# First weights prepared in the opening stage, weight work spread over iterations, and mLSTM products in the last four iterations of an attention loop

## The chip, the cores and the metric

One core of a Trainium2 chip runs one launch of the kernel. The metric is device time in microseconds: the median of three runs before the change is 1974.31 (1969.93 to 1977.7). Smaller is better.

## The reference

The reference is one layer of a diffusion backbone: 1024 latent tokens and 256 context tokens, 1024 channels. What matters here is its first half. A normalised and modulated `h` is projected once; the parts feed two token mixers, and a sigmoid gate weighs each:

```
h  = modulate(rms_norm(x, norm1_w), sh1, sc1);  hc = the same for ctx
aq, ak, av, mq, mk, mv, mo, mg, ga, gm = split(h @ w_in)
att = windowed_gqa(rope(norm(aq)), rope(norm(ak)), av, k_ctx, v_ctx, sink)   # 16 heads, 4 KV heads, window 128
ml  = readout(bidirectional mLSTM(mq, mk, mv, gates mg; states from ctx), mo) # 4 heads, chunks of 128
y   = sigmoid(ga) * (att @ w_branch_att) + sigmoid(gm) * (ml @ w_branch_ml)
x   = x + g1 * (y @ w_out);  then a convolutional SwiGLU with its own residual
```

All of it is fp32. The kernel holds fp32 accuracy on TensorE by splitting an operand in a high and a low half and taking three products: high by high, high by low, low by high.

## The kernel before, in words

The stages run one after another: `stage_startup` (modulation vectors, context projections, and `h` in transposed halves `hH`, `hL`), `stage_attention`, `stage_mlstm`, and a tail with the merge and the feed-forward part. Outside the attention loop a planner sets the order of instructions on each engine with its own cost model; `tc.issue_after(x)` makes what follows on an engine stand behind `x`. The attention loop is under `tc.manual_schedule()`: there each engine runs in the order written, and a wait on one instruction holds all that is behind it on the same engine. Loads of weights all go through SP's queue, in order too.

**Weights.** A weight becomes two 16-bit halves in four steps (class `ScaledWeights`, L84 to 159): load of fp32 quarters (`raw`, L100), squares summed on ACT (`square`, L111), a total across partitions by a product with ones on PE, a reduction on DVE, a scale with a power on POOL (`total`, L118 to 121; `back`, L125 and L126), and the split, on POOL in three instructions for each piece: scale (L140), cast (L141), subtract (L142). A group's attention weight has four quarters of 128x768 (the first 128x800), a gate weight two halves of 128x512.

**Attention loop.** Its 36 iterations `n` are a pipeline over 32 pairs (group of heads `g` = n // 8, block of 128 tokens `b`). In iteration n, the projection `pq` of pair n (24 products, L686), the transposes of pair n-1 (L772), the scores, maxima, exponentials and low halves of pair n-3 (four heads; L822 to L825 on PE, L830 and L846 on DVE, L838 to L841 on ACT), and the value products `po` of pair n-4 stand interleaved. Between them stand 24 products of a gate tile `g` (j = 0 at n = 0, then j = n - 2 up to 31, two tiles for each of 16 gate weights). In an iteration, DVE reduces the squares of `pq` (L717 on ACT, L724 on DVE) to row factors, POOL finishes them (L725 to L727), DVE rotates the key by them (L750), POOL adds (L761, L762). `pv_end` (L887, POOL) multiplies the finished output by norms that come back from DRAM (`R`). The reciprocals of the softmax sums are transposed on PE (L861, `norm_turn`), ahead of the gate products.

The weight work has its own timetable in the loop. Gate weight c is loaded at the end of iteration 2c - 1, squared in 2c, totalled in 2c + 1, and both halves are split in 2c + 1; its first tile is due in 2c + 2. The attention weight of group g = 1 to 3 is loaded in iterations 8(g-1) and 8(g-1) + 2, squared in the iterations after each, totalled at n % 8 = 4, and split two quarters there and two at n % 8 = 6. `weight_back` (L642) also makes scalars for the values on POOL and takes a reciprocal on DVE (L654). Before the loop, the first attention weight and the first gate weight go through all four steps, and the loop's first projection and gate tile wait for them. In iterations 32 to 35 there is no projection, in 34 and 35 no gate tile.

**mLSTM start.** `prepare(0)` loads, squares and totals the weights `w_ml` and `w_mlqo` of head 0, `gate_math` is a chain of small operations for the gates (from L1219 to L1313), `load_kv(0)` splits `w_ml` on ACT and DVE, `proj_kv(0)` makes keys and values `kv` for eight latent blocks (24 products each, L162 to L164), and `trans_k`, `states` (L1365 on), `proj_q` and `core` follow.

Of the kernel before, what the change touches and what calls it, by code (L numbers as in the profile page):

```python
# [18 lines left out]
P = 128  # L19
D = 1024  # L20
# [69 lines left out]
class ScaledWeights:  # L90
# [4 lines left out]
    def __init__(self, E, tc, ctx):  # L95
        self.E, self.nc = E, E.nc
        pool = lambda name, bufs: ctx.enter_context(tc.tile_pool(name=name, bufs=bufs, reuse_waits="tile"))
        self.rp, self.hp, self.lp, self.sp = pool("w2_raw", 4), pool("w2_h", 8), pool("w2_l", 8), pool("w2_s", 1)

# [239 lines left out]
def stage_startup(E, at):  # L339
# [3 lines left out]
    with ExitStack() as st:  # L343
# [28 lines left out]
        def norm(i, t, late=None):  # L372
            junk = wp.tile([P, D], F32, tag="junk", name=f"xj{i}", bufs=1)
# [189 lines left out]
        for i in range(4):  # L563
# [6 lines left out]
            for k in range(0, KT, 2):  # L570
# [8 lines left out]
                if i == 1 and k < 4:  # L579
                    for c in range(2 * k, 2 * k + 4, 2):  # L580
                        X[4 + c // 2] = load(NCB + 4 + c // 2)
            if i == 2:
                at.tables(cs)
# [18 lines left out]
def stage_attention(E, st, at):  # L602
# [12 lines left out]

    norm_d = E.dr.tile([NKV * NB, 512], F32, name="norm_d")
# [6 lines left out]
    WSRC = [(A["w_att0"], 400)] + [(A["w_att"][g], 384) for g in range(3)]  # L623
# [19 lines left out]
    def weight_back(g):  # L643
        f = RAW["wf", g]
        w2.back(f)
# [11 lines left out]
    def gate_load(c, i):  # L657
        raw = fp.tile([P, 4, P], F32, tag="fr", name=f"fr{c}_{i}")
# [283 lines left out]
    for k2 in range(4):  # L942
        weight_load(0, k2)
        weight_square(0, k2)
    weight_total(0, tp_tile("wt0"))
    weight_back(0)
    for k2 in range(4):
        weight_split(0, k2)
    for i in range(2):
        gate_load(0, i)  # L950
        gate_square(0, i)
    gate_total(0, tp_tile("gt0"))
    gate_back(0)
    for i in range(2):
        gate_split(0, i)
    for i in range(2):
        mod_fetch()

    def squares(n, i):
        if n % 2 == 0 and 1 <= n // 2 < 16:  # L960
            gate_square(n // 2, i)
        if n % 8 in (1, 3) and n // 8 < 3:
            weight_square(n // 8 + 1, n % 8 - 1 + i)

    prior, tile_done, out_done = None, None, None
    with tc.manual_schedule():
        for n in range(LAST):
# [5 lines left out]
            if tile_done:  # L973
                gate_act(*tile_done)
# [3 lines left out]
            squares(n, 0)  # L978
# [8 lines left out]
            ps, new = proj(*now) if now else (None, Products())  # L987
# [5 lines left out]
            if n % 8 == 6 and n // 8 < 3:  # L993
                weight_split(n // 8 + 1, 2)
                weight_split(n // 8 + 1, 3)
# [9 lines left out]
            new.some(len(new.todo))  # L1005
            if prior:
                prior.norm_turn(pt[0:4, 384:512])
            c = n // 2 if n % 2 and 1 <= n // 2 < 16 else None
            if c:
                gate_total(c, ps[:, 448:])  # L1010
            heavy = n // 8 + 1 if n % 8 == 4 and n // 8 < 3 else None
            if heavy:
                weight_total(heavy, ps[:, 448:])
            j = TILES.get(n)
            fps, gate = gate_tile(j) if j is not None else (None, Products())
            gate.some(8)
# [5 lines left out]
            if c:  # L1022
                for i in range(2):
                    gate_split(c, i)
            if heavy:
                weight_split(heavy, 0)
# [4 lines left out]
            sq = values_act(*now, ps) if now else None  # L1031
# [15 lines left out]
            if c:  # L1047
                gate_back(c)
            if heavy:
                weight_back(heavy)  # L1050
                weight_split(heavy, 1)
# [4 lines left out]
            squares(n, 1)  # L1056
            gate.some(24)
            if j is not None:
                tile_done = j, fps
# [14 lines left out]
            if n % 2 and 1 <= (n + 1) // 2 < 16:  # L1074
                for i in range(2):
                    gate_load((n + 1) // 2, i)
            if n % 8 in (0, 2) and n // 8 < 3:
                for i in range(2):
                    weight_load(n // 8 + 1, n % 8 + i)
            prior = S  # L1080
        if tile_done:
            gate_act(*tile_done)
# [1293 lines left out]
```

## Time and profile before

| what | us |
|---|---|
| median of the runs shown | 1974.31 |
| the profiled execution, its own time | 1971.89 |
| its span, first to last instruction | 1969.9 |
| first and last L717 (one for each projection) | 119.6, 637.3 |
| first and last attention product (L686) | 102.5, 697.3 |
| PE, DVE, ACT, POOL busy, share of the span | 93%, 72%, 54%, 25% |
| mean granted TensorE clock | 0.969 |

PE's busy share is the mean of stages with different limits, and matmuls are pipelined, so it is not PE at its peak. POOL's 25% lies nearly all in the first third of the span. The chain of waits that ended last runs over PE for 67% of the span.

### The profile page before, as it was taken

The page shows a single profiled execution, that of the slowest core. Times are in us where ns is not written, and L with a number is a line of the kernel's source. Part 1 is how long each engine was busy: PE and PEld are TensorE (multiplying, and loading weights), DVE is VectorE, ACT ScalarE, POOL GpSimd, SP SyncE. Part 2 cuts the span into 40 slices and gives each one's busy share as a digit, 9 for nine tenths or more (in the row PEclk, how much of TensorE's full clock was granted, in tenths as well). Part 3 has the DMA queues.
Part 4 walks back from the last instruction along what each step waited for, and adds up shares of the span by engine and source line. Part 5 has one row for each costly group of instructions (what it writes and reads, how often), then busy time and mean ns, then how long its engine had stood idle before and what let it go on. Part 6 is the DMA issues. An engine that isn't in the chain of part 4 may idle for free.

```text
span 1969.9 us, 27867 instructions
## 1 busy us (share of the span) xinstructions
PE 1826.1 (93%) x9121; PEld 1318.9 (67%) x9121; DVE 1423.7 (72%) x2874; ACT 1069.9 (54%) x2199; POOL 493.7 (25%) x739
## 2 busy tenths in 40 slices
PE   7858888988899789999999999999999999999999
PEld 4824554545555446565656888787888888888887
DVE  3826766766767657586768778769998988997565
ACT  4716666666667655656445656246544444454441
POOL 2476647647554224131302002000000000000000
PEclk9979999999999889999999999999999999999999
DMA  9625775777767770516243993632355444489851
GB/s 353 194 80 118 158 154 122 158 161 149 162 145 156 157 216 22 182 63 208 74 150 112 371 346 101 244 130 76 124 186 204 181 169 168 166 305 354 293 180 64
DMA packets 301936, 342.46 MB, mean 174 GB/s; under 512 B 175824, under 2 KB 200416, under 8 KB 298976
## 3 DMA queue, kind: packets, MB, share of 16 engines
q1 hardware_dynamic: 287392, 314.47, 52.7%
q10 hardware_dynamic: 14400, 26.22, 4.1%
q8 instruction: 72, 1.18, 0.3%
q14 instruction: 72, 0.59, 0.1%
HBM read 224.61 MB, written 76.16 MB: 153 GB/s over the span
## 4 chain that ended last, share of the span: by engine, by line
PE 67%; ACT 7%; DMA 7%; POOL 7%; DVE 6%; issue 5%; SPq 1%; ACTq 0%; POOLq 0%; DVEq 0%
PE g L686 5%; PE pa L1954 4%; PE pa L1956 4%; PE pa L1955 4%; PE pq L686 4%; PE po L686 3%; DMA fr<-in_w_g 2%; PE dx L1954 2%; PE dx L1956 2%; PE dx L1955 2%; PE pb L1956 2%; PE pb L1955 2%; PE pb L1954 2%; PE yb L1954 2%; PE yb L1956 2%
## 5 line engine op out<-in xcount | busy, mean ns | idle before, releaser
L830 DVE CUSTOM_DVE_ANT_0 s<-s,maskA,nsink 128x640 f32<-128x640 f32 (+1 forms) x128 | 117.3, 916 | 78.9 <-PE s L825 78.4
L846 DVE TENSOR_TENSOR P<-s,P 128x640 f16<-128x640 f32 (+1 forms) x128 | 100.6, 786 | 25.9 <-ACT s L841 25.7
L686 PE MATMUL pq<-wha,hH 128*128 128x384 f16 (+1 forms) x256 | 90.1, 352 | 31.2 <-DVE t L750 18.5
L686 PE MATMUL g<-hH,fh 128*128 128x512 f16 x256 | 102.3, 400 | 3.1 <-POOL fh L141 3.1
L840 ACT ACTIVATE P<-s,st 128x640 f16<-128x640 f32 (+1 forms) x128 | 98.2, 768 | 8.5 <-DMA T<-P 4.0
L686 PE MATMUL g<-hH,fl 128*128 128x512 f16 x256 | 101.6, 397 | 0.6 <-POOL fl L142 0.6
L686 PE MATMUL g<-hL,fh 128*128 128x512 f16 x256 | 102.1, 399 | 0.0
L686 PE MATMUL pq<-wla,hH 128*128 128x384 f16 (+1 forms) x256 | 89.5, 350 | 4.7 <-POOL wla L142 4.7
L841 ACT ACTIVATE s<-s,st 128x640 f32<-128x640 f32 (+1 forms) x128 | 93.9, 734 | 0.0
L686 PEld LDWEIGHTS <-hH 128*128 128x128 f16 x512 | 51.2, 104 | 63.6 <-issue 21.1
L162 PE MATMUL kv<-whkv,hH 128*128 128x384 f16 x256 | 85.3, 333 | 4.8 <-DVE VL L56 4.8
L686 PE MATMUL pq<-wha,hL 128*128 128x384 f16 (+1 forms) x256 | 89.5, 349 | 0.0
L838 ACT ACTIVATE st<-st,shift 128x1 f32<-128x1 f32 x128 | 37.2, 291 | 94.9 <-DVE st L830 94.5
L822 PE MATMUL s<-KA,QT 128*128 128x384 f32 (+1 forms) x128 | 64.1, 501 | 25.3 <-DVE P L846 16.7
L163 PE MATMUL kv<-wlkv,hH 128*128 128x384 f16 x256 | 85.2, 333 | 0.4
L164 PE MATMUL kv<-whkv,hL 128*128 128x384 f16 x256 | 84.9, 331 | 0.0
L686 PEld LDWEIGHTS <-fh 128*128 128x128 f16 x512 | 49.6, 104 | 51.5 <-issue 7.8
L1365 POOL TENSOR_SCALAR kwh<-k,gcall 128x128 fp32r<-128x128 f32 x72 | 32.1, 450 | 177.6 <-PE dC L163 72.7
L2092 ACT ACTIVATE cv<-ua,vecT 128x1024 f32<-128x1024 f32 x22 | 27.4, 1245 | 85.3 <-DVE ua L2065 85.3
L1954 PE MATMUL dx<-dwh,dfh 128*128 128x512 f32 (+1 forms) x176 | 68.3, 388 | 0.0
L1956 PE MATMUL dx<-dwh,dfl 128*128 128x512 f32 (+1 forms) x176 | 68.3, 388 | 0.0
L1955 PE MATMUL dx<-dwl,dfh 128*128 128x512 f32 (+1 forms) x176 | 68.2, 387 | 0.0
(670 smaller groups left out, 6204.1 us busy)
## 6 DMA issues: line engine op xcount, KB each, us to landing
ur<-in_w_up SPq DMA_DIRECT2D x22, 1024.0 KB
wmb<-in_w_modB SPq DMA_DIRECT2D x48, 256.0 KB
f_d<-cv SPq DMA_DIRECT2D x22, 512.0 KB
wm<-in_w_modA SPq DMA_DIRECT2D x16, 512.0 KB
fr<-in_w_g SPq DMA_DIRECT2D x32, 256.0 KB
drf<-fs_d SPq DMA_DIRECT2D x15, 512.0 KB
drw<-wt_d SPq DMA_DIRECT2D x14, 512.0 KB
w1b<-in_w_cx SPq DMA_DIRECT2D x16, 388.0 KB
```

The costliest lines, as they stand in the source:

```text
L162: nc.tensor.matmul(ps, lh[:, ls], rh[:, rs], start=start and i == 0, stop=False)
L163: nc.tensor.matmul(ps, lh[:, ls], rl[:, rs], start=False, stop=False)
L164: nc.tensor.matmul(ps, ll[:, ls], rh[:, rs], start=False, stop=stop and i == n - 1)
L686: nc.tensor.matmul(self.ps, x, w, start=self.i == 0, stop=self.i == self.n - 1)
L822: nc.tensor.matmul(s[:, self.lat], q, G[g]["KA"][:, ks], start=True, stop=False)
L830: nc.vector.tensor_tensor_reduce(e, e, self.mask, scale=self.ss[:, h : h + 1], scalar=nsink[:, hh : hh + 1], op0=ALU.add, op1=ALU.min, acc ...
L840: nc.scalar.activation(two[:, :W], e, AF.Exp, bias=m, scale=-1.0)
L841: nc.scalar.activation(e, e, AF.Exp, bias=m, scale=-1.0, accum_out=st4[:, 4 + h : 5 + h])
L846: nc.vector.tensor_tensor(two[:, W : 2 * W], self.e[h], two[:, :W], op=ALU.subtract)
L1954: nc.tensor.matmul(ps, lh, rh, start=start and i == 0, stop=False, skip_group_check=True)
L1955: nc.tensor.matmul(ps, lh, rl, start=False, stop=False, skip_group_check=True)
L1956: nc.tensor.matmul(ps, ll, rh, start=False, stop=stop and i == n - 1, skip_group_check=True)
```

## The change

- `stage_startup`: the first attention weight's loads are traced in step 1 of the context loop, its squares there too, its total and its POOL splits at the start of step 2 (splits behind the last norm factor). The first gate weight is loaded in step 2, squared there and totalled in step 3. The rotary tables move from the end of step 2 to the end of step 1. The norms' junk tile is 16 bit.
- Before the loop: only the scalars of group 0, the splits of gate weight 0, three gate loads and one weight load are left.
- In the loop each piece has its own iteration. Gate weight c: loads at the end of 2c - 5 and 2c - 4, squares in 2c - 3 and 2c - 2, total in 2c - 1, splits in 2c and 2c + 1. Group g, with a = 8(g-1): loads in a - 1 to a + 2, squares in a + 1 to a + 4, total in a + 4, splits in a + 5 to a + 8; the last quarter stands at the head of POOL's work in its iteration, the other pieces behind `pv_end`.
- `w_ml` and `w_mlqo` of head 0 join the timetable: `w_ml` as a fifth group (split in 29 to 32), `w_mlqo` loaded in 30 to 33, squared in 32 to 35, totalled in 35.
- `norm_turn` moves behind the first eight gate products.
- In iterations 32 to 35 the place of the projection, and in 34 and 35 that of the gate tile too, is taken by the 24 products of one of the mLSTM's blocks 0 to 5; ACT copies the result to SBUF (`kv0`, held until `proj_kv(0)` is done), and `proj_kv(0)` reads it from there. Blocks 6 and 7 stay.

```diff
@@ stage_startup, context loop (step i, piece k)
+                w2 = E.w2
+                if i == 1 and k == 2:
+                    E.raw0 = [w2.raw(A["w_att0"][:, j : j + 2, :], 400, f"a0_{j // 2}") for j in range(0, KT, 2)]
+                if i == 1 and k == 4:
+                    q0 = w2.sums("a0")
+                if i == 1 and k >= 4:
+                    for j in (k - 4, k - 3):
+                        w2.square(q0, j, E.raw0[j], "a0")
+                if i == 2 and k == 0:
+                    E.f0 = w2.total(q0, 4, tp_tile("wt0"), "a0")
+                    w2.back(E.f0)
+                    E.W0 = []
+                    with tc.issue_after(E.factor.ins):
+                        for j in range(4):
+                            h, lo = w2.halves(400, f"a0_{j}")
+                            w2.split_pool(E.raw0[j], E.f0, h, lo)
+                            E.W0 += [(h[:, jj], lo[:, jj]) for jj in range(2)]
...
+            if i == 1:
+                at.tables(cs)
             if i == 2:
-                at.tables(cs)
                 context_squares()
@@ stage_attention
+    def early(j, ps):
+        todo = [
+            (x[:, sl(j * P, P)], w)
+            for (xh, xl), (wh, wl) in zip(hT, W1[NKV])
+            for x, w in ((xh, wh), (xh, wl), (xl, wh))
+        ]
+        return ps, Products(ps[:, :384], todo)
+
+    def early_act(j, ps):
+        E.kv0[j] = E.kvp.tile([P, 384], F32, name=f"kv0_{j}")
+        copy_act(nc, E.kv0[j], ps[:, :384], scale=RAW["wf", NKV][:, 4:5])
+
+    def gate_slots(c):
+        load = [2 * c - 5, 2 * c - 4]
+        square = [max(2 * c - 3, 0), 2 * c - 2]
+        return load, square, 2 * c - 1, [2 * c, 2 * c + 1]
+
+    def weight_slots(g):
+        if g > NKV:
+            return [30, 31, 32, 33], [32, 33, 34, 35], 35, []
+        a = 8 * (g - 1)
+        return [a + k - 1 for k in range(4)], [a + k + 1 for k in range(4)], a + 4, [a + k + 5 for k in range(4)]
...
-            ps, new = proj(*now) if now else (None, Products())
+            splits = list(jobs(n, 3))
+            for kind, c, i in splits:
+                if kind == "w" and i == 3:
+                    weight_split(c, i)
+            ps, new = proj(*now) if now else early(n - N, mm_tile(f"kv0_{n - N}"))
...
+            elif n >= N + 2:
+                fps, gate = early(n - N + 2, E.fl_tile(f"kv0_{n - N + 2}"))
+            gate.some(8 if valued != seq[-1] else 24)
             if prior:
                 prior.norm_turn(pt[0:4, 384:512])
@@ stage_mlstm, proj_kv
+            elif h == 0 and j - NCB in E.kv0:
+                kv = E.kv0[j - NCB]
+                copy_act(nc, k, kv[:, 0:DQK], scale=DQK ** -0.5)
+                vs[j] = v_tiles(h, j, kv[:, 128:384])
```

More of the change, by code (lines that the diff above doesn't have):

```diff
@@ L622, in stage_attention @@
     w2 = E.w2
-    WSRC = [(A["w_att0"], 400)] + [(A["w_att"][g], 384) for g in range(3)]
+    WSRC = [(A["w_att0"], 400)] + [(A["w_att"][g], 384) for g in range(3)] + [(A["w_ml"][0], 384), (A["w_mlqo"][0], 384)]
     def weight_load(g, k2):
@@ L1021, in stage_attention @@
                 mod_sum()
[L1022 to L1026, printed above, removed]
             if S:
@@ L1046, in stage_attention @@
                 context_values(g)
[L1047 to L1051, printed above, removed]
+            for kind, c in totals(n):
+                (gate_back if kind == "g" else weight_back)(c)
             if S:
```

122 lines of the change are left out of this document (75 added, 47 removed).

## The prediction

> **What bounds the kernel now.** I read the windows first (busy time by stretch), then who waits for whom, then the timelines where a stretch loses time. In a windows row the fields are: stretch, its length, busy us (and instructions) of PE, PEld, DVE, ACT, POOL, then granted clock, DMA share and GB/s.
>
> ```profile
> 73.00:81.00 8.00, 6.84 (x42) 6.24 (x42) 7.71 (x8) 6.44 (x11) 8.00 (x8) 1.00 0.81 216
> 81.00:93.00 12.00, 12.00 (x76) 11.85 (x75) 8.86 (x15) 10.47 (x19) 0.21 (x1) 1.00 0.56 185
> 93.00:110.00 17.00, 4.90 (x21) 2.37 (x20) 4.38 (x11) 2.85 (x6) 14.82 (x17) 0.70 0.46 129
> 110.00:130.00 20.00, 10.89 (x32) 4.18 (x32) 3.13 (x12) 0.64 (x2) 19.30 (x22) 0.66 0.04 14
> 590.57:604.21 13.64, 13.64 (x79) 8.56 (x78) 11.12 (x29) 11.01 (x29) 4.86 (x8) 1.00 0.83 153
> 572.34:590.57 18.23, 16.60 (x88) 9.98 (x86) 11.10 (x32) 11.05 (x28) 11.48 (x14) 0.91 0.65 131
> 188.00:647.00 459.00, 402.80 (x2147) 241.29 (x2145) 314.85 (x803) 299.83 (x746) 274.98 (x345) 0.96 0.71 151
> 647.00:698.00 51.00, 36.73 (x147) 20.30 (x147) 31.97 (x69) 30.47 (x68) 9.26 (x17) 0.74 0.73 160
> 698.00:753.00 55.00, 49.28 (x278) 28.33 (x276) 29.41 (x83) 32.72 (x79) 15.91 (x45) 0.96 0.53 167
> ```
>
> Three places lose PE time. From 93 to 130 POOL is full and PE mostly waits: POOL alone splits the first weights. In the loop, two neighbouring iterations of the same work take 13.64 and 18.23; the fast one keeps PE busy all the time, so 13.64 is PE's own pace. And from 647 to 698, where the projections have ended, PE works 36.73 of 51 at clock 0.74.
>
> ```profile
> 72.71 0.55 POOL L384 TENSOR_TENSOR rs<-ss,expo 128x1 f32<-128x1 f32 x1
> 73.23 0.20 POOL L321 TENSOR_SCALAR nsink<-sink 128x16 f32<-128x16 f32 x1
> 80.02 1.19 POOL L329 TENSOR_TENSOR TB<-cs,qw 128x256 f32<-128x256 f32 x1
> 95.66 2.85 POOL L140 TENSOR_SCALAR wra<-wra,wfa 128x800 f32<-128x800 f32 x1
> 118.74 1.57 POOL L140 TENSOR_SCALAR fr<-fr,wfg 128x512 f32<-128x512 f32 x1
> 122.63 0.61 PE L686 MATMUL g<-hH,fh 128*128 128x512 f16 x1 [3.08 <-POOL fh L141]
> ```
>
> So the first gate product stands at 122.6, behind POOL's run of weight splits (95.66 to about 118) and then the gate's.
>
> In the loop the waits say why (us in total, times, longest):
>
> ```profile
> PE qt L861 <- ACT KA L47: 25.3, 15, 3.2
> PE pq L686 <- DVE t L750: 18.5, 12, 2.0
> PE s L822 <- DVE P L846: 15.3, 5, 4.1
> DVE t L750 <- POOL ss L727: 34.3, 14, 3.6
> DVE vs L654 <- POOL vs L652: 9.7, 2, 4.9
> ACT wjg L111 <- DMA fr<-in_w_g: 24.8, 12, 3.5
> ACT wja L111 <- DMA wra<-in_w_att: 15.0, 4, 3.9
> ```
>
> One slow iteration shows the chain, on POOL and then PE:
>
> ```profile
> 572.92 1.58 POOL L140 TENSOR_SCALAR fr<-fr,wfg 128x512 f32<-128x512 f32 x1
> 576.41 1.58 POOL L140 TENSOR_SCALAR fr<-fr,wfg 128x512 f32<-128x512 f32 x1
> 580.00 0.28 POOL L725 TENSOR_SCALAR ss<-ss,vs 128x5 f32<-128x5 f32 x1
> 582.10 0.72 POOL L761 TENSOR_TENSOR qf<-qf,t 128x256 f32<-128x256 f32 x1
> 583.29 1.26 POOL L887 TENSOR_TENSOR o<-o,R 64x512 f32<-64x512 f32 x1
> 582.67 0.32 PE L686 MATMUL pq<-wha,hH 128*128 128x384 f16 x1 [1.63 <-DVE t L750]
> ```
>
> Both halves of a gate weight are split in one odd iteration (2 x 3.5), the row factors `ss` queue behind them, DVE's L750 waits for these, and PE's next projection for L750. In even iterations ACT stands at a square whose weight was only just requested (L111 on DMA), and PE's L861 pays. Every fourth of eight iterations, `weight_back`'s L654 stops DVE.
>
> **The change, part by part.** All sums are against the profiled execution, 1971.9 (span 1969.9); the median of the runs shown, 1974.3, is 2.4 above it.
>
> *Opening.* Loads, squares, total and POOL splits of the first attention weight move into the context loop; the split is pinned behind the last norm factor (72.71+0.55). A quarter of a weight costs POOL 4.9:
>
> ```profile
> 316.34 2.21 POOL L140 TENSOR_SCALAR wra<-wra,wfa 128x768 f32<-128x768 f32 x1
> 321.28 0.28 POOL L725 TENSOR_SCALAR ss<-ss,vs 128x5 f32<-128x5 f32 x1
> ```
>
> Four quarters: 73.3 + 19.6 = 92.9. The opening L140 took 2.85 where the loop's takes 2.21, so up to 29% more, 98.6; I take 96. The rotary tables (POOL 73.2 to 81.2) are now traced a step earlier and pinned to the norms before; they should run from about 65, ahead of the second half's norms, which may come 5 late: the context products cover that, since the latents' second half is first needed at iteration 3. Then the value scalars (between 0 and the 4.9 of L654's wait; I take 2) and one gate half, 3.5: first gate product at 101.5 instead of 122.6, **-21**. The gate weight's own load, squares and total are off the path, done by then. ACT's six early squares only move: its share before was similar in place.
>
> POOL under DVE costs something:
>
> ```profile
> L54 DVE TENSOR_TENSOR hL<-hf,hH x16: 671/687/1231, 54.2 to 95.7; 128x512 f16<-128x512 f32 x16
> ```
>
> While POOL runs the tables, this subtraction goes from 0.69 to 1.23, and PE loses 1.16 of 8.00; 19.6 more of POOL would lose 2.8. It is covered: context ends near 96, 24 products at 0.163 make 99.8, and the gate waits until 101.5 anyway. Without that cover it costs the 2.8. The Trainium skill, SBUF — State Buffer, section "SBUF: two separate sides", says more: an exclusive lock, the loser blocked for the other's whole instruction. By that, some 15 such subtractions would each wait about half of a 2.2 instruction, an estimated 16, so context and projection would end near 113 and the opening bring 10 instead of 21; the trace's longest case, 1.23, speaks for the smaller price.
>
> Bounds of the opening: -10 (PE, in order, meets the two totals L118 before late weights) to -24.
>
> *Filling, iterations 0 to 5.* Same stalls, partly: the last two intervals there were 15.9 and 20.4 against 14 to 15 after: **-7** (0 to -12).
>
> *Steady loop.*
>
> ```profile
> 191.75 0.44 ACT L717 ACTIVATE sq<-pq 128x320 f32<-128x320 f32 x1
> L717 ACT ACTIVATE sq<-pq x32: 436/437/440, 119.6 to 637.3; 128x320 f32<-128x320 f32 x32
> ```
>
> L717 runs once an iteration: 26 intervals from 191.75 to 637.3, 445.6, or 17.1 each. After the change:
> - Ten ordinary iterations (one gate half each, squares one to two iterations after their load, the transpose L861 behind eight gate products, 1.7 of cover): PE's 13.64 plus what that interval lacks (the small sums of the modulation): 14.2.
> - Fourteen iterations with a weight quarter too. POOL: gate half 3.5, quarter 4.9, factors 2.1 (580.00 to 582.10), rotary sums 1.2, L887 1.3, a total's two about 0.8: 13.8, as much as PE. Quarter 3 now falls into the very iteration that first uses it: PE reaches it about 4 in, POOL about 5, so 1 is lost, with the gate products and two score products queued behind. I take 15.2.
> - Two with `weight_back` (12, 20): L654 still waits, but without the quarter (about 1.7) ahead: 17.
>
> Sum 10 x 14.2 + 14 x 15.2 + 2 x 17 = 388.8, gain 56.8. DVE and ACT, 11.1 and 11.0 per iteration, would then be near 75%, DMA near 0.8, as in the fast interval; since no row shows all of them so for long, I take **-52**. Bounds: all at 13.64, -91; fourteen heavy and two totals as before and half of the 2.9 elsewhere, -15.
>
> The slow interval is 4.6 longer with only 1.63 of wait: its clock is 0.91. The Trainium skill, TensorE: Matmul & The Clock Gate, Part 1, has the clock fall after an idle window of about 3.4; by it stalls under 2 would cost only themselves and the loop would bring about 40. The trace disagrees (0.91 beside 1.63 idle), and I keep 52.
>
> *Last four and the mLSTM start.*
>
> ```profile
> 699.48 0.33 PE L162 MATMUL kv<-whkv,hH 128*128 128x384 f16 x1
> 711.34 0.33 PE L163 MATMUL kv<-wlkv,hH 128*128 128x384 f16 x1
> 700.55 0.21 DVE L1219 COPY fin<-gtile 128x80 f32<-128x80 f32 x1
> 715.57 0.38 PE L118 MATMUL wtw_mlqo<-wqw_mlqo,ones 128*128 128x4 f32 x2 [3.90 <-ACT wjw_mlqo L111]
> 729.50 0.68 DVE L1313 COPY gcall<-gcols 128x512 f32<-128x512 f32 x1
> L162 PE MATMUL dC<-VH,kwh x72: 278/356/472, 739.9 to 1060.4; 128*128 128x258 f32 x72
> ```
>
> 73 steps in 11.86 are 0.163 each, 3.9 for a block of 24. Six of the eight blocks move (four in the projection's place, two in the gate's): 23.4. From 647 to 698 PE does 36.73 x 0.74 = 27 at full clock; with 23.4 it is just full, and in order I expect 3 more (0 to 8). After it, the gate arithmetic is the path: 700.55 to 730.2, 29.6, of which the wait for w_mlqo's squares (3.9, and PE's row of work around it, about 6 in all) goes, since that weight is now prepared in iterations 30 to 35. PE had covered this chain with the products now gone; what covers it are two blocks (7.8) and the q products. The first state product then starts at 698 + 3 + 2.5 + 24 = 727 instead of 739.9: **-13**. Bounds -24 (PE always finds work) and +3 (chain unchanged, stage 8 longer, six extra ACT copies). Eight loads (w_ml, w_mlqo) move in SP's queue to iterations 23 to 33, between the score transposes; buffers are free two iterations, for w_mlqo one, before they are asked for.
>
> At nothing: the 16-bit junk tile, six `fr` buffers, new pools, other columns of the bank.
>
> Sum: 21 + 7 + 52 + 13 = 93; 1971.9 - 93 = 1879, with half of the 2.4: **1880**.
>
> **The rivals.**
> - *POOL sets the pace.* Heavy iterations stay at 17, the loop brings 20: 1912. For it: 13.8 of POOL beside PE's 13.6, in order. Against: POOL was idle in even iterations (4.86).
> - *Opening does not move*: splits are placed late, or totals stall PE; 3 instead of 21: 1898.
> - *Gate arithmetic stands bare*: the tail gives +3: 1896.
> - *Everything at PE's pace*: 91, 12, 24, 20: 1825 to 1845.
> - *Slower*: POOL and DVE stretch each other in the heavy iterations. DVE's subtraction stretched 1.79-fold, POOL's L140 1.29-fold. With a factor f on 13.8 and 1.5 of waiting, the 16 iterations with a quarter cost 16 x (13.8 f + 1.5 - 17.1) against 72 gained elsewhere (21, 13, and 13 ordinary ones at 2.9). It decides from f = 1.46; at 1.55 the time is 1992. Against: the loop's L140 took only 2.21.
> - *Gains cancel*: within 0.5%.
>
> **How the numbers follow.** Forecast 0.50 (its own range 1860 to 1900), POOL's pace 0.18, opening 0.07, bare gate arithmetic 0.08, PE's pace 0.05, slower 0.08, cancelled 0.04. The range 1845 to 1930 leaves out the last two and the far ends. About 0.5%, 10 us, is what a measurement can tell: faster 0.88, same 0.04, slower 0.08.
>
> **What would show it.** Right: first gate product near 101; L750 on L727 and L111 on DMA gone from the waits; L717 intervals even, near 15, in the loop; clock near 1.00 there; dC before 730. Wrong: POOL full in iterations 13 to 16 with L727 still awaited; PE idle before L118 at 65 to 90; PE idle after 700.

## The result, and the profile after

The changed kernel takes 1882.77 (median of four runs, 1877.94 to 1885.33) against 1973.33 before (1969.93 to 1977.7): a ratio of 0.9537, 95% interval 0.951 to 0.9565, or 91 us. 1880 was predicted. Its profiled execution took 1877.94 (span 1876.1, clock 0.988), 94.0 less than the profiled one before, and is the fastest of the four; the points below are read against that one. In the changed file the lines moved: the square of the projection is L755 (was L717), attention products are L724 (L686), the rotary products L788 (L750), the row factors L763 to L765, POOL's splits L141 to L143, `weight_back`'s reciprocal L692, `norm_turn` L899, the first state product L163.

Windows of the changed kernel, with columns as in the prediction: two stretches of the opening, the steady loop from the sixth to the last L755, and from there to the attention's end.

```profile
60.00:73.00 13.00, 10.93 (x64) 9.39 (x63) 11.24 (x18) 12.03 (x24) 8.88 (x11) 0.94 0.98 328
81.00:93.00 12.00, 10.39 (x58) 9.32 (x57) 10.76 (x12) 8.34 (x14) 12.00 (x8) 1.00 0.84 255
...
174.66:561.32 386.66, 371.88 (x2082) 224.29 (x2080) 308.42 (x778) 291.55 (x723) 283.40 (x346) 1.00 0.84 172
561.32:624.00 62.68, 58.84 (x334) 35.09 (x333) 39.33 (x88) 41.62 (x98) 23.67 (x48) 1.00 0.89 186
```

The steady loop of the kernel before, cut at the same two instructions:

```profile
191.75:637.33 445.58, 391.44 (x2085) 234.63 (x2084) 305.83 (x780) 291.27 (x727) 265.06 (x332) 0.95 0.72 152
```

The 26 intervals fell from 445.58 to 386.66, by 58.9. Of that, 39.4 is idle time of PE (445.58 - 391.44 = 54.1 before, 14.8 after) and 19.6 is busy time for the same products, at clock 1.00 instead of 0.95. POOL did 18.3 more work there (11.8 of it belongs to w_ml's quarters: the run x_last, without them, has 271.56) and is at 73%.

Who waits for whom in the loop of the changed kernel (us in total, times, longest):

```profile
PE s L860 <- DVE P L884: 9.5, 7, 2.9
PE pq L724 <- POOL wla L143: 2.2, 2, 1.1
DVE QT L830 <- PE qt L899: 47.4, 26, 3.0
DVE vs L692 <- POOL vs L690: 6.4, 2, 3.2
```

The three waits that the prediction began from (L861 on ACT's `KA`, `pq` on L750 on the row factors, the squares on DMA) are gone. PE's wait for DVE's low halves is not: in these 26 intervals it was 8.3 before and is 9.5 (the 15.3 in the prediction's row reaches back into the filling). A new one has come: DVE stands before its half of the query transposes, 1.8 in each iteration, for `norm_turn`. Before, the same wait was small:

```profile
DVE QT L792 <- PE qt L861: 4.3, 10, 0.6
```

The opening, from the timelines of PE (the last context product first), POOL and ACT:

```profile
100.63 0.34 PE L165 MATMUL cx<-w1h,hcL 128*128 128x388 f32 x1
...
70.25 1.30 POOL L327 TENSOR_TENSOR TA<-cs,qw 128x256 f32<-128x256 f32 x1 [1.13 <-DMA cs<-in_rope]
78.67 3.09 POOL L141 TENSOR_SCALAR wra<-wra,wfa 128x800 f32<-128x800 f32 x1
101.63 0.57 POOL L122 TENSOR_TENSOR wfg<-wfg,expo 128x1 f32<-128x1 f32 x1
102.29 4.39 POOL L141 TENSOR_SCALAR fr<-fr,wfg 128x512 f32<-128x512 f32 x2
108.88 1.85 POOL L142 CAST fh<-fr 128x512 f16<-128x512 f32 x2
109.77 0.61 PE L724 MATMUL g<-hH,fh 128*128 128x512 f16 x1 [4.31 <-POOL fh L142]
113.26 0.63 ACT L112 ACTIVATE wjg<-fr 128x512 bf16<-128x512 f32 x1 [10.38 <-DMA fr<-in_w_g]
```

The first gate product stands at 109.8, not at 101.5. The splits began at 78.67, behind the tables. POOL came to the tables only when all four norm factors were done, at 69.13, and their load, requested at 62.57, let them begin at 70.25. Both gate halves were scaled before either was cast; and ACT stood 10.4 at a square whose weight was only requested at 109.71.

The mLSTM's start: a product that waits, start and end of the gate arithmetic, first state product, first score product.

```profile
632.32 0.48 PE L163 MATMUL kv<-wha,hH 128*128 128x384 f16 x1 [4.38 <-DVE o L1135]
638.43 0.19 DVE L1291 COPY fin<-gtile 128x80 f32<-128x80 f32 x1
653.48 0.69 DVE L1385 COPY gcall<-gcols 128x512 f32<-128x512 f32 x1 [0.21 <-PE gcols L1382]
L163 PE MATMUL dC<-VH,kwh x72: 277/358/472, 654.7 to 971.9; 128*128 128x258 f32 x72
L163 PE MATMUL S<-qh,kh x32: 272/276/411, 658.6 to 948.3; 128*128 128x128 f32 x32
```

And the first score product of the kernel before:

```profile
L162 PE MATMUL S<-qh,kh x32: 272/276/410, 752.5 to 1036.8; 128*128 128x128 f32 x32
```

From the last square of a projection to this product: before 752.5 - 637.33 = 115.2, after 658.6 - 561.32 = 97.3. From there to the end both take as long, 1217.4 before and 1217.5 after, but only in sum. The state products (`dC`, whose last one starts at 1060.4 before and at 971.9 after) show it: from the first score product to the last state product it is 307.9 before and 313.3 after, and from that one to the end 909.5 and 904.2. Counted from the last square to the last state product, this part brought 12.5 (423.1 to 410.6). What follows is touched by no part of the change, and the other kernels measured below, with the same code there, took 903.2 to 909.2 for it, so the last 5.3 can't be put down to the change.

The 94.0 therefore lie so: opening to the first gate product 12.9 (122.63 to 109.77), from there to the sixth square 4.2, steady loop 58.9, last four iterations and mLSTM start 17.9 at the first score product, of which 12.5 are left at the last state product.

### The profile page after: what moved, and what is told of

Read it like the earlier page. It is cut to its first block, busy times and chain, and to the rows that moved or that the text cites. A ratio compares the mean times of both kernels' runs of the same rounds, so it can differ in the third digit from the quotient of the medians.

```text
span 1876.1 us, 27851 instructions
## 1 busy us (share of the span) xinstructions
PE 1796.9 (96%) x9121; PEld 1306.9 (70%) x9121; DVE 1428.9 (76%) x2870; ACT 1070.1 (57%) x2201; POOL 517.0 (28%) x751
## 4 chain that ended last, share of the span: by engine, by line
PE 75%; DVE 7%; DMA 5%; POOL 5%; ACT 4%; issue 2%; SPq 0%; ACTq 0%; DVEq 0%; POOLq 0%
PE g L724 7%; PE pq L724 5%; PE pa L2027 4%; PE pa L2028 4%; PE pa L2029 4%; PE yb L2027 2%; PE yb L2029 2%; PE po L724 2%; PE yb L2028 2%; PE dx L2027 2%; PE dx L2029 2%; PE dx L2028 2%; PE pb L2028 2%; PE pb L2029 2%; PE pb L2027 2%
## 5 line engine op out<-in xcount | busy, mean ns | idle before, releaser
L724 PE MATMUL g<-hH,fh 128*128 128x512 f16 x256 | 98.3, 384 | 4.3 <-POOL fh L142 4.3
L884 DVE TENSOR_TENSOR P<-s,P 128x640 f16<-128x640 f32 (+1 forms) x128 | 100.6, 786 | 2.2 <-ACT s L879 2.2
L724 PE MATMUL g<-hH,fl 128*128 128x512 f16 x256 | 98.2, 383 | 1.1 <-POOL fl L143 1.1
L724 PE MATMUL g<-hL,fh 128*128 128x512 f16 x256 | 98.1, 383 | 0.0
L724 PE MATMUL pq<-wla,hH 128*128 128x384 f16 (+1 forms) x256 | 85.8, 335 | 2.2 <-POOL wla L143 2.2
L724 PE MATMUL pq<-wha,hL 128*128 128x384 f16 (+1 forms) x256 | 86.4, 337 | 0.0
L724 PE MATMUL pq<-wha,hH 128*128 128x384 f16 (+1 forms) x256 | 86.3, 337 | 0.0
L724 PEld LDWEIGHTS <-hH 128*128 128x128 f16 x608 | 57.9, 100 | 36.7 <-issue 3.2
L724 PEld LDWEIGHTS <-fh 128*128 128x128 f16 x512 | 48.1, 101 | 50.4 <-POOL fh L142 4.7
L2165 ACT ACTIVATE cv<-ua,vecT 128x1024 f32<-128x1024 f32 x22 | 27.4, 1245 | 84.6 <-DVE ua L2138 84.6
L830 DVE TENSOR_TENSOR QT<-qt,QT 64x256 fp32r<-64x256 f32 x64 | 27.0, 422 | 56.5 <-PE qt L899 53.9
L860 PE MATMUL s<-KA,QT 128*128 128x384 f32 (+1 forms) x128 | 56.2, 439 | 14.1 <-DVE P L884 14.1
L163 PE MATMUL kv<-whkv,hH 128*128 128x384 f16 x192 | 63.3, 330 | 6.1 <-DVE VL L56 6.0
L47 ACT ACTIVATE dfh<-drf 128x512 fp32r<-128x512 f32 x55 | 34.3, 628 | 59.1 <-PE dx L2028 26.5
```

What stands on the lines that cost most here:

```text
L47: return nc.scalar.activation(out, in_, AF.Copy, scale=scale)
L163: nc.tensor.matmul(ps, lh[:, ls], rh[:, rs], start=start and i == 0, stop=False)
L724: nc.tensor.matmul(self.ps, x, w, start=self.i == 0, stop=self.i == self.n - 1)
L860: nc.tensor.matmul(s[:, self.lat], q, G[g]["KA"][:, ks], start=True, stop=False)
L884: nc.vector.tensor_tensor(two[:, W : 2 * W], self.e[h], two[:, :W], op=ALU.subtract)
```

## The experiments

Each run is the changed kernel with one thing edited (the last two with several). Times are ratios to the kernel before, run on the same chip; "+x" is the difference of the ratio to 0.9537, times 1972. The changed kernel was timed beside other runs of the kernel before, with an interval of its own (about 3 to each side), so differences of a few us are read from the traces. Five of the kernels (the changed one, x_open, x_slip, x_slip2 and y_sums) have the very same loop, and it took 386.4 to 389.9 in them: a difference of the loop below 3.5 says nothing.

### The opening put back (x_open)

```diff
-    W1[0] = E.W0
-    RAW["wf", 0] = E.f0
+    for k2 in range(4):
+        weight_load(0, k2)
+        weight_square(0, k2)
+    weight_total(0, tp_tile("wt0"))
...
+    for k2 in range(4):
+        weight_split(0, k2)
...
```

The blocks for these weights in the context loop are gone, and the tables stand again in its step 2.

> The opening alone is put back (first weight and first gate weight loaded, squared, summed and split after the context products, tables one step later); loop and last four as in the changed kernel (1882.8). Theory from the two traces: the change won 12.9 at the first gate product and the loop passes that on, some filling stalls return with it: +13 to +17, so 1896 to 1900, first gate product near 122. Rival, the prediction's own size: +21 to +28 (1904 to 1911). Rival, only the first attention square counts (it came 5.7 earlier): +6, 1889.

Measured: 1894.18, ratio 0.9615 (0.9594 to 0.9635): +15. Its timeline on PE and its loop:

```profile
121.56 0.39 PE L693 MATMUL g<-hH,fh 128*128 128x512 f16 x1 [2.86 <-POOL fh L142]
...
184.78:574.66 389.88, 374.95 (x2082) 226.10 (x2080) 306.39 (x778) 291.66 (x723) 284.46 (x347) 0.99 0.83 172
```

The first gate product moved by 11.8, the sixth square by 10.1; the loop's 3.2 lie within its scatter. From the first score product on, where this edit changes nothing, the trace is 8.3 longer than the changed kernel's, so the +15 is read from the medians alone. The opening is worth what the traces said and not the 21 of the prediction.

### Why the opening gave 12.9: splits only behind the context (x_slip, x_slip2)

In the first form the split stood behind a mark on the planner's order:

```diff
-                    with tc.issue_after(E.factor.ins):
...
+                if i == 3 and k == 6:
+                    E.W0 = []
+                    with tc.issue_after(wts.rest.ins):
+                        for j in range(4):
...
```

> In the opening the first attention weight is loaded, squared and totalled in the context stage as in the changed kernel, but POOL splits it only behind the last context weight's subtraction. Theory A (POOL's splits stretch DVE's subtractions, 0.68 to 2.35, and so the context products): the context products end 4 to 7 earlier than in the changed kernel, near 94 to 97, and no subtraction is over 1.4. Theory B (the added loads and squares crowd DMA and ACT): the end stays within 2 of the changed kernel's 101. In both the first gate product comes late, near 122 to 126, and the time is 10 to 20 over the changed kernel.

Measured: 1875.96 in one run. POOL's timeline shows that the mark moved nothing:

```profile
79.95 3.08 POOL L141 TENSOR_SCALAR wra<-wra,wfa 128x800 f32<-128x800 f32 x1
```

It is a second look at the changed kernel and says nothing of A or B. The second form makes the order a need: the factor is taken from the last weight's remainder.

```diff
-                            w2.split_pool(E.raw0[j], E.f0, h, lo)
...
+                    nc.vector.scalar_tensor_tensor(
+                        late[:, 2:3], w[-1][1][:, 0:1].bitcast(F32), 0.0, E.f0[:, 2:3], op0=ALU.mult, op1=ALU.add
+                    )
...
+                        w2.split_pool(E.raw0[j], late, h, lo)
...
```

> As in the run before, but the split of the first attention weight now reads a factor that is only made from the last context weight's remainder (0 times one element of it, added to the factor), so POOL cannot start before the context's last subtraction. Theory A (POOL's splits stretch DVE's subtractions, and these the context products): context products end 4 to 7 earlier than the changed kernel's 101, at 94 to 97, no subtraction of 128x776 over 1.4 beside them; the first attention product then waits for the split, near 101, with its last quarter near 118, and the first gate product is near 122. Theory B (the added loads and squares crowd DMA and ACT): the context's end stays within 2 of the changed kernel's. Time: 10 to 16 over the changed kernel (about 1879 here) in both.

Measured: 1891.62 in one run, 13 over the 1879 taken for the changed kernel there; first gate product at 120.21. Its windows, and the last context product:

```profile
60.00:73.00 13.00, 10.56 (x61) 9.36 (x60) 11.28 (x18) 12.99 (x26) 8.10 (x11) 0.92 0.90 311
...
81.00:93.00 12.00, 11.77 (x70) 11.40 (x69) 8.81 (x15) 8.96 (x16) 0.38 (x1) 1.00 0.71 220
...
98.65 0.34 PE L165 MATMUL cx<-w1h,hcL 128*128 128x388 f32 x1
```

The last context product ends at 98.99 here and at 100.97 in the changed kernel. In the kernel before it was this one, ending at 93.38:

```profile
93.04 0.34 PE L164 MATMUL cx<-w1h,hcL 128*128 128x388 f32 x1
```

Of the 7.6 of slip, 2.0 go with the splits and 5.6 stay without them: theory B for most. From 60 to 73 PE does 10.56 here and 10.93 in the changed kernel where it did 13.00 before, with ACT at 12.99 and 12.03 (11.87 before) and DMA at 0.90 and 0.98 (0.88 before): the first weight's loads and squares stand there between the context's own. That these make up the 5.6 is argued from the windows; the earlier tables are in both kernels too, and none of the three was taken out alone. POOL's part is seen from 81 to 93, PE 11.77 against 10.39, and in the mean of DVE's big subtraction, this run first, the changed kernel second:

```profile
L78 DVE TENSOR_TENSOR w1l<-w1b,w1h 128x776 fp32r<-128x776 f32 x15 | 14.8, 998 | 1.9 <-ACT w1h L47 1.9
```
```profile
L78 DVE TENSOR_TENSOR w1l<-w1b,w1h 128x776 fp32r<-128x776 f32 x16 | 18.5, 1171 | 0.0
```

Sixteen times 0.17 is 2.8, the size that the prediction gave to POOL under DVE.

### The place of the gate splits (x_both, x_both2)

In x_both both halves are split right after the total, in 2c - 1; in x_both2 in 2c + 1, as in the kernel before. In both the two calls stand behind `mod_sum`, ahead of the row factors.

```diff
@@ x_both2
-        return load, square, 2 * c - 1, [2 * c, 2 * c + 1]
+        return load, square, 2 * c - 1, [2 * c + 1, 2 * c + 1]
...
             if n < 3 or n % 2:
                 mod_sum()
+            for kind, c, i in splits:
+                if kind == "g":
+                    gate_split(c, i)
```

> Both halves of a gate weight are split in the odd iteration, right after its total and ahead of the row factors, as before; all else as in the changed kernel. Theory (the place of the splits on POOL sets the loop): the wait of DVE's rotary product for the row factors returns in about 13 iterations at 1.5 to 2.5 each, +20 to +33, 1903 to 1916. Rival (the loop was won by the earlier loads and squares, POOL has room either way): within 5 of 1882.8.

Measured: 1953.55, ratio 0.9905 (0.9882 to 0.9927): +73, twice the theory's most. The rows of its loop show a wait that was not meant:

```profile
185.64:639.54 453.90, 396.92 (x2082) 234.88 (x2080) 298.54 (x778) 294.61 (x724) 284.24 (x345) 0.94 0.70 147
...
DVE t L788 <- POOL ss L765: 59.6, 13, 4.8
PE pq L724 <- DVE t L788: 45.2, 12, 4.1
POOL fh L142 <- PE g L724: 25.9, 22, 3.0
```

Two iterations early, the split needs buffers of halves that PE is still reading (four `fh` tiles): POOL waits 25.9 in the middle of a split, with the row factors behind it. So the place was tried again without that.

> Both halves of a gate weight are split in the odd iteration in which the second half is split now (one later than in the run with both splits right after the total), ahead of the row factors, where the kernel before had them: the buffers of the split halves are then free, so POOL no longer waits for PE's gate products (25.9 in the earlier run). All else as in the changed kernel (about 1879 on this chip). Theory (the place of the splits on POOL sets the loop): every odd iteration has 7.0 of splits ahead of the factors, PE waits 1.5 to 4 for the rotary product 13 times, with the slower clock +25 to +55: 1904 to 1934. Rival (the +75 of the earlier run came from the buffers, not from the place): within 10 of the changed kernel.

Measured: 1907.36, ratio 0.9677 (0.9663 to 0.9692): +28, at the lower end of the theory and far outside the rival. The loop is 27.4 longer:

```profile
179.34:593.44 414.10, 378.63 (x2082) 226.89 (x2080) 300.12 (x778) 293.75 (x724) 284.20 (x345) 0.98 0.77 161
...
DVE t L788 <- POOL ss L765: 34.3, 13, 3.6
PE pq L724 <- DVE t L788: 22.9, 12, 2.8
```

The wait of DVE for the row factors is back: 34.3 in 13 times, where the kernel before has 31.6 in 13 times in its 26 intervals (the 34.3 of the prediction's row is of a longer stretch). So is PE's wait for DVE, 22.9 against 18.5. This part of the cause is shown.

### The distance of a square from its load (x_load, x_pairs)

In x_load every load is one iteration later and every square at the top of the iteration behind it. In x_pairs both loads of a gate weight stand in 2c - 3 and its squares at the top and late in 2c - 2; the attention weights' likewise.

```diff
@@ x_load
-        load = [2 * c - 5, 2 * c - 4]
+        load = [2 * c - 4, 2 * c - 3]
...
@@ x_pairs
-        load = [2 * c - 5, 2 * c - 4]
-        square = [max(2 * c - 3, 0), 2 * c - 2]
+        load = [2 * c - 3, 2 * c - 3]
+        square = [2 * c - 2, 2 * c - 2]
...
```

> Every weight is loaded one iteration later and squared at the top of the next iteration, straight behind its load, as before; splits as in the changed kernel. Theory (ACT's wait for the weight's load held the transposes back, 24.8 + 15.0 of ACT waits and 25.3 of PE waits before): +10 to +25, 1893 to 1908, with ACT's squares waiting on DMA again. Rival (ACT has slack at 75% and the eight gate products ahead of the transposes cover it): within 4 of 1882.8.

Measured: 1932.18, ratio 0.9804 (0.9789 to 0.9819): +53. The theory's direction, twice its size; here 23 squares of gate weights wait for their load in the loop, where the kernel before had 12.

```profile
ACT wjg L112 <- DMA fr<-in_w_g: 85.2, 23, 4.9
PE qt L899 <- ACT KA L47: 32.7, 17, 4.9
```

> Loads and squares in the pattern before: both pieces of a weight are requested at the end of one iteration, the first squared at the top of the next, the second late in it; splits stay spread as in the changed kernel. Theory (ACT waiting for a load at the top of an iteration holds the transposes): about half as many squares stand behind their load as in the run with all of them so (+53), so +20 to +30: 1899 to 1909. Rival (that run's loss came from its own request order on SP's queue): within 8.

Measured: 1907.00, ratio 0.9667 (0.9643 to 0.969): +26, as the theory had it. Loop:

```profile
179.91:592.13 412.22, 379.27 (x2082) 226.81 (x2080) 304.60 (x778) 288.22 (x723) 281.79 (x345) 0.98 0.78 163
...
ACT wjg L112 <- DMA fr<-in_w_g: 48.3, 12, 5.2
PE qt L899 <- ACT KA L47: 22.8, 14, 2.6
```

ACT is at 70% in this loop and is still what PE waits for: its mean share hides a stand of 4 at the top of an iteration.

### The last four without mLSTM products (x_last)

```diff
-            ps, new = proj(*now) if now else early(n - N, mm_tile(f"kv0_{n - N}"))
+            ps, new = proj(*now) if now else (None, Products())
...
-        for g in range(1, NKV + 2):
+        for g in range(1, NKV):
...
```

`prepare(0)`, `load_kv(0)` and `proj_kv(0)` are as before.

> The last four iterations hold no mLSTM products again, and the two mLSTM weights of the first head are made after the attention, as before; opening and loop as in the changed kernel. Theory: what the traces give for this part, 17.8 (15 to 22): 1898 to 1905. Rival (the gate arithmetic stood bare in the changed kernel and gave it back): +3 or less, 1882 to 1886.

Measured: 1894.40, ratio 0.9611 (0.9593 to 0.9629): +15. But not all of it lies where the theory had it. Its loop, SP's waits from 414 to 475, SP's timeline from 449, ACT, and the first and last score and state products:

```profile
174.28:568.50 394.22, 375.12 (x2080) 224.86 (x2078) 306.86 (x776) 291.29 (x723) 271.56 (x335) 0.99 0.81 168
...
SPq L103 <- POOL wfg L121: 11.9, 2, 6.9
...
449.03 0.70 SPq L926 DMA_DIRECT2D attT_d<-o  x1
456.36 0.39 SPq L103 DMA_DIRECT2D wrw_ml<-in_w_ml  x1
456.84 1.41 SPq L885 DMA_TRANSPOSE T<-P  x1
...
461.36 0.79 ACT L878 ACTIVATE P<-s,st 128x640 f16<-128x640 f32 x1 [2.58 <-DMA T<-P]
...
L163 PE MATMUL S<-qh,kh x32: 273/276/411, 678.0 to 961.5; 128*128 128x128 f32 x32
L163 PE MATMUL dC<-VH,kwh x72: 278/357/472, 665.5 to 985.1; 128*128 128x258 f32 x72
```

The planner puts the first requests for `w_ml` on SP's queue in the middle of the loop; there such a request waits for POOL, whose splits free the four raw tiles (SP stands from 449.7 to 456.36), the score transposes stand behind it, and ACT waits for these. The loop is 7.6 longer, and it is these stands that lengthen it: the intervals behind iterations 22 and 23 are 18.58 and 19.31, where the changed kernel has 14.08 and 15.80. The kernel before has the same requests (at 459.05, 468.33 and 491.40); what they cost there was not tried apart. From the last square to the first score product, 568.50 to 678.0, it is 109.5, 12.2 more than in the changed kernel. 19.8 in all, of which about 7 were given back later: 6.2 up to the last state product (307.1 from the first score product, where the changed kernel has 313.3) and 1.0 behind it. So the moved products are themselves worth 6.0 at the last state product (416.6 from the last square, against 410.6), and the requests that they took off SP's queue 7.6.

### The sums that hold the gate arithmetic (y_sums)

```diff
-            if h == 0 and j - NCB in (0, 3):
-                branch_sums()
...
-            for _ in range((3, 4, 3)[h]):
+            for _ in range((4, 4, 4)[h]):
```

> The two sums of branch weights that stood among the first mLSTM products (their loads on ACT's queue, their sums on DVE) move to the end of the first and third head; all else as in the changed kernel. Theory (they held the gate arithmetic back: it began 14.4 after the attention's end, before the change 3.3): the gate arithmetic begins 4 to 8 after the attention, the first state product comes 5 to 11 earlier, time -4 to -10. Rival (the weights' and context's loads set this stage, or the heads give it back): within 2.

Measured: 1876.52, ratio 0.9521 (0.9507 to 0.9536): -3, not told apart from no change.

```profile
632.56 0.20 DVE L1289 COPY fin<-gtile 128x80 f32<-128x80 f32 x1
L163 PE MATMUL dC<-VH,kwh x72: 277/357/778, 647.4 to 971.4; 128*128 128x258 f32 x72
```

The gate arithmetic began 5.9 earlier and the first state product came 7.3 earlier, as the theory had it; the last one came at 971.4 against 971.9. The heads gave the rest back (its span is 0.4 below the changed kernel's), and the rival's ending holds. Part of the start's cost is no cost at the end.

### The transpose of the normalisers put back (x_turn)

```diff
             new.some(len(new.todo))
+            if prior:
+                prior.norm_turn(pt[0:4, 384:512])
             for kind, c in totals(n):
...
             gate.some(8 if valued != seq[-1] else 24)
-            if prior:
-                prior.norm_turn(pt[0:4, 384:512])
```

> The transpose of the normalisers (with the bank that waits for ACT's copies of the query transposes) stands again ahead of the eight gate products and of the weight totals, as before; all else as in the changed kernel. Theory (the eight products, 8 x 0.216 = 1.7, cover ACT's copies): PE waits at that transpose in most iterations, 0.3 to 1 each, +5 to +15. Rival (with the squares no longer behind their loads ACT is in time anyway): within 4.

Measured: 1865.35, ratio 0.9446 (0.9422 to 0.9469): **18 us faster** than the changed kernel by the ratios, and 12.8 by the two traces (spans of 1863.3 and 1876.1). The theory was wrong in sign, and the rival, which allowed a gain of 4, was far too small.

```profile
173.69:551.92 378.23, 369.58 (x2081) 226.86 (x2080) 305.82 (x781) 290.19 (x724) 283.56 (x347) 1.00 0.86 176
...
DVE QT L830 <- PE qt L899: 3.0, 4, 1.4
```

In this loop PE does not wait for `KA` at L899 at all: with the squares far from their loads, ACT is in time, and nothing needs the cover of eight gate products. What they did was to make DVE wait: its half of the query transposes reads the tile (`pt`) into which L899 writes, and in the changed kernel it stands behind that write, so it stood 47.4 for it, 1.8 an iteration, and PE's scores waited for DVE's low halves (L860 on L884, 9.5 in the changed kernel, 4.9 here). The loop gains 8.4, the stretch from its end to the first state product 5.1 more, of which 3.3 are left at the last one (407.3 from the last square, against 410.6).

### All of it together (y_all, y_turn)

```diff
-        gate_split(0, i)
+    gate_split(0, 0)
+    with tc.issue_after(E.low.ins):
+        gate_split(0, 1)
...
-                if kind == "w" or n == 0 and i == 0:
+                if kind == "w":
...
-        nc.vector.reciprocal(t[:, 5:6], t[:, 3:4])
+        LATER.append((t[:, 5:6], t[:, 3:4]))
...
+            while LATER:
+                nc.vector.reciprocal(*LATER.pop())
             mod_end()
```

y_all has y_sums' edit beside these; y_turn has x_turn's instead.

> The changed kernel with four places mended: the first gate half is finished on POOL before the second is begun; the first square of gate weight 1 stands late in iteration 0 and its load ahead of the modulation rows on SP's queue; the last reciprocal of the value scalars (DVE waits 3.2 for it) stands at the iteration's end; the two sums of branch weights leave the first mLSTM products, as in the run with this alone (-3). Theory: first gate product near 108 (109.8), square of iteration 1 near 118 (123.5), so -4 to -5; intervals 12 and 20 back to 15, -4 to -6; sums -3: together -8 to -14, 1865 to 1871 here. Rival (later stages give these back as they did most of the sums' 7): -3 or less, 1876.

Measured: 1867.57, ratio 0.9456 (0.9431 to 0.948): -16, a little beyond the theory. Its trace is 6.4 shorter than the changed kernel's, and up to the last state product 10.9 (961.0 against 971.9), as the theory had it. Its loop:

```profile
172.04:554.67 382.63, 371.60 (x2078) 223.88 (x2077) 306.63 (x778) 291.41 (x723) 284.86 (x347) 1.00 0.84 174
```

The sixth square is 2.6 earlier, and the loop 4.0 shorter (the intervals behind iterations 12 and 20 went from 18.63 and 16.94 to 14.68 and 14.62).

> The changed kernel with the transpose of the normalisers back ahead of the gate products (as in the run that had this alone, ratio 0.9446 against 0.9537), the first gate half finished on POOL before the second, the first square of gate weight 1 late in iteration 0, and the value scalars' last reciprocal at the iteration's end; the sums of branch weights stay where the changed kernel has them. Theory (the transpose's place cost DVE 1.8 an iteration, the reciprocal 3 to 4 in three iterations, the opening's order 2.6, and these do not cover each other): 0.9446 less 6 to 8 us, ratio 0.940 to 0.942, about 1857. Rival (PE's own work of 13.6 to 14 an iteration is reached by the transpose alone, the rest finds no room): ratio 0.943 to 0.946.

Measured: 1857.38 (1853.52 to 1860.83), ratio 0.9426 (0.9401 to 0.9451): the fastest of all, 22 us below the changed kernel by the ratios and 20.5 by the traces. Between the theory's and the rival's figures, and the interval holds both; the trace shows that the parts do add in the loop (374.14, which is the 8.4 of x_turn and 4.1 more below 386.66):

```profile
170.45:544.59 374.14, 368.25 (x2080) 225.83 (x2079) 305.26 (x780) 290.45 (x723) 284.91 (x347) 1.00 0.86 178
```

PE is busy 98% of this loop, 14.4 an iteration against the 13.64 that the prediction named as its pace.

## Why the prediction was right, point by point

**The sum.** 93 was predicted, 94.0 came (91 by the medians). Four terms of 21, 7, 52 and 13 stand against 12.9, 4.2, 58.9 and 17.9: the total is better than its parts. Up to the loop 11 too much was forecast, from the loop on 12 too little; that these cancel is luck, and 5.3 of the 94.0 lie behind the last state product, where the change does nothing.

**Opening, -21, came as -12.9.** The step that failed is the start: the tables "should run from about 65, ahead of the second half's norms". They ran from 70.25, behind all four norms, and the splits, which the prediction had straight behind the norms, stood behind the tables: 78.67 instead of 73.3, 5.4 late. The length of the four quarters was right (22.7 taken, 22.6 measured). Behind them the prediction had 5.5 for scalars and one gate half; it took 8.5, since the gate's total (0.9) and the other half's scaling stood between. The context's slip, 2.8 predicted and called covered, was 7.6; the runs showed that POOL's splits under DVE cost 2.0, and that 5.6 come without them, by the windows from the added loads and squares, which the prediction had at nothing ("ACT's six early squares only move"). It stayed covered: PE waited 4.31 for the gate half in any case. By the exclusive lock of the Trainium skill, SBUF — State Buffer, section "SBUF: two separate sides", the opening would have brought 10, nearer to 12.9 by number. But its mechanism is not what these runs show: an exclusive wait for whole instructions would have slipped the context by an estimated 16, and without the splits it ended only 2.0 earlier. In the changed kernel's trace one big subtraction of DVE (80.84, 0.95 long) runs without delay inside POOL's scaling of 78.67 to 81.76.

**Filling, -7, came as -4.2**, with a wait of ACT that was not seen (10.38, at the first square of gate weight 1).

**Steady loop, -52, came as -58.9.** The raw sum was 388.8, and 386.66 came. Its parts held too: sorted by the iteration in which they begin, the ordinary intervals came as 14.4 (14.2 forecast), those with a weight quarter as 14.8 (15.2) and the two with `weight_back` as 17.8 (17). Both causes are shown, each undone alone: the splits' place is worth 27.4 of loop (x_both2), the squares' distance from their loads 25.6 (x_pairs), of 58.9. The waits named as the signs went and came back with them. The discount of 5 for DVE, ACT and DMA "since no row shows all of them so for long" was not needed: DMA stood at 0.84 for the whole loop. One step was wrong in sign and hidden by the sum: "the transpose L861 behind eight gate products, 1.7 of cover". No cover was needed, and the place cost 8.4 (x_turn). With it, the rest of the change (the spread of the attention weights' quarters, `weight_back` without a quarter ahead, the requests that left SP's queue, 7.6 in x_last) would have to bring about 14, if the parts add; only the last of these was seen in a run, where the last four iterations were undone with it. By the idle window of about 3.4 in the Trainium skill, TensorE: Matmul & The Clock Gate, Part 1, stalls shorter than it would have cost only themselves, and the loop would have brought about 40, the prediction's estimate; PE's busy time for the same products fell by 19.6 as the clock rose from 0.95 to 1.00, which this window does not give, and 58.9 came.

**Last four and mLSTM start, -13, came as -9.2 at the first state product** that the prediction named (102.6 behind the last square before, 93.4 after) **and as -17.9 at the first score product**, of which 12.5 are left at the last state product. Undone alone it is 12.2 at the first score product and 6.0 at the last state product (x_last); the other 5.7 and 6.5 came from outside this part and were not tried apart. The last four took 2.7 longer (59.97 to 62.68), as was said (3). Two steps were off in opposite ways: the gate arithmetic took 15.7 instead of the 24 taken for it, but began 14.4 after the attention and not 2.5. The request on SP's queue, which the prediction priced at nothing, held 7.6 of the loop.

**The rivals.** POOL did not set the pace: in the changed kernel's loop DVE no longer waits for the row factors. POOL and DVE did not stretch each other there either: the scaling L141 of a quarter took 2.207 (2.21 in the prediction's row), so the factor that a slower kernel needed was not there:

```profile
L141 POOL TENSOR_SCALAR wra<-wra,wfa 128x768 f32<-128x768 f32 x14 | 30.9, 2207 | 0.0
```

The gate arithmetic did begin late, and PE stood 4.38 ahead of it for DVE, but the chain itself was shorter. PE's own pace was not reached by this change; y_turn comes within 0.75 an iteration of it.

**The signs.** Waits gone, clock 1.00 and the mean interval (14.87) came as listed. The intervals are not even (13.4 to 18.6 in ACT's timeline), and the first gate product came 8 later than listed.

## What to carry to other kernels

A piece of side work in a tight loop has three prices that its busy time doesn't show: what stands behind it on its own engine, how far it stands from the transfer that feeds it, and which buffer or bank it holds for another engine. Move one piece at a time and look who newly waits: here one line of a change that was right as a whole cost 13 us by the traces and 18 by the ratios, its row (47.4 of DVE waits at 26 of 26 iterations) stood in the profile, and its cure took one move. A stage's earlier start is worth only what the next stage can use: 7.3 won at the first state product came to 0.4 of span.

## What was not expected of the hardware

- A third of the loop's gain is clock, not waits: 19.6 of 58.9. In x_both, with clock 0.94, PE was busy 25.0 longer than in the changed kernel for as many products. The 39.4 of idle time that went came with half as much again in clock.
- The DMA engines stood at a mean share of 0.84 to 0.86 for some 380 us, while PE was busy for 96% to 98% of them.
- In x_last a request that waited for a buffer held the later requests of SP's queue: with stands of up to 6.9 its loop was 7.6 longer.
